# Sixteen gate projections as eight pairs of seven half-size products, with a shared minimum and undivided maps in branch A

## The chip, the cores and the metric

The kernel runs on one core of one Trainium2 chip. The metric is the device time of one execution in microseconds. The engines are named as in the profile: PE multiplies matrices (PEld is its loading of weights), DVE, ACT and POOL work elementwise, SP issues DMAs. A line number such as L735 is a line of the kernel before.

## The reference

An encoder block over 1024 tokens and 16 meta tokens, width 1024, in float32. What matters here:

```
proj = rms_norm(h) @ w_in              # queries, keys, values of A and B, then gates ga and gb (1024 columns each)
# branch A, 4 heads, two maps each, 1040 keys:
attn = softmax(q1 k1^T / 8 + bias) - lam * softmax(q2 k2^T / 8 + bias)
y_a  = rms_norm(attn @ v) * gain
# branch B: 8 heads over a window of 128 keys on either side, plus the meta tokens
merged = sigmoid(ga) * (y_a @ w_ba) + sigmoid(gb) * (y_b @ w_bb)
h = h + merged @ w_o;  h = h + swiglu(rms_norm(h));  out = rms_norm(h)
```

The gates are two products of a 1024 x 1024 activation with a 1024 x 1024 weight. The tokens' bias in branch A is minus a slope times the distance; to the meta tokens the distance counts as zero.

## The kernel before

**Precision.** A float32 operand is split into a high part (ACT, L115) and the rest (POOL or DVE, L116), each in a reduced float format, and a product is three matmuls: high times high, high times rest, rest times high. The activation lies transposed in `hT_hi` and `hT_lo`, eight blocks of 128 features by 1040 tokens.

**Stages.** (1) Input norm and the first projections. (2) The window attention of branch B (`attend_b`, L358 to L406: scores on PE, minimum on DVE, exponential on ACT, the division on POOL at L370, transposes, values), with the projections of branch A's queries, keys and values put between its steps. (3) Branch A with the gates. (4) The branch products (L679), the product with `w_o`, and the feed-forward part.

**Branch A** works through 32 tiles of 128 queries (4 heads of 8). `scores_a` computes, for map 1 and then map 0, three chunks of 352, 352 and 336 keys (two matmuls each, L735), each in its own PSUM bank out of five (`SC`). DVE adds slope times distance and takes the running minimum (L741; the last chunk in two instructions, 16 meta keys and 320 others). ACT takes the exponential with the sum of the row (L746), DVE the reciprocal (L747). POOL scales map 1 by its reciprocal and minus lambda (L749), DVE joins both maps (L752), POOL copies the meta columns (L753). One tile later PE transposes the joined map (L764), ACT and DVE split it (L767, L768), and for every second tile PE multiplies it with the values (L777). `normed_a` squares the result, sums it on PE (L790), and applies the norm (L792 to L799).

**Order.** In stage 3 PE's order is written by hand. Each tile walks through the string `SLOTS`: `s` is one score chunk, `t` one group of transposes, `n` one step of the values or the norm of an earlier pair of tiles, and `g` one gate step, three matmuls of 512 columns. `G_FIRST` gate steps stand ahead of the first tile, `G_HEAD` ahead of the first tile of the three other heads; in both places `load_a` issues the loads of the head's queries, keys and values, whose buffers are single. `HOLD` gate steps are kept for the end: there each call of `step_tail` is followed by `fill(3)`, and `fill(1000)` issues what is left. A gate column block (128 columns by 1024 tokens) is 48 matmuls in two chunks (`project_steps`, L227), copied out by ACT (L686) and stored (L687); its weight is loaded at L188. The order on the other engines comes from a planner that simulates the program. SP issues almost all loads and stores in one order.

## Time and profile before

| what | value |
| --- | --- |
| time of three runs | 1429.1, 1431.18, 1431.73 us; median 1431.18 us |
| profiled execution | span 1427.5 us; the page gives no other time of it, so 1.6 to 4.2 us of the runs' times lie around the span |
| granted TensorE clock | 0.999 |
| stage 2, about | 60 to 293 us |
| stage 3, about | 293 to 621 us (first score matmul at 313.7 us) |
| branch products from | 621.4 us |

A row of a group reads: line, engine, operation, output and inputs, shapes, count, then total busy time and the mean duration of one, then how long the engine was idle before them and for whom. A row of the timeline or of the chain begins with its start and its duration. Matmuls overlap in the pipeline, so the duration of one matmul is not its cost: the distance from start to start is.

### The profile page before, as it was taken

The numbers are of one execution on the slowest core, as the hardware profiler recorded it, in microseconds if no ns is written. First come the engines' busy times: TensorE is split into PE (matmuls) and PEld (weight loads), VectorE is DVE, ScalarE is ACT, GpSimd is POOL, SyncE is SP. The second block draws the span as 40 slices with busy tenths as digits, with TensorE's granted clock in tenths as the row PEclk, the third lists the DMA queues.
The fourth block names the chain that finished last, engine by engine and source line by source line (L and its number), as shares of the span: only waits on it lengthen the run. The fifth ranks groups of instructions, "written<-read, shape, count | busy, mean of one in ns | idle before, by whom it ended". The sixth has DMA issues, their size and how long they took to land.

```text
span 1427.5 us, 20915 instructions
## 1 busy us (share of the span) xinstructions
PE 1418.5 (99%) x7279; PEld 1222.2 (86%) x7279; DVE 907.8 (64%) x1808; ACT 673.0 (47%) x1276; POOL 463.7 (32%) x462
## 2 busy tenths in 40 slices
...
GB/s 240 95 124 104 99 115 106 84 257 48 149 75 157 68 156 68 34 307 242 143 123 82 207 83 145 152 99 104 110 104 96 97 108 99 357 188 141 125 126 148
DMA packets 159018, 191.55 MB, mean 134 GB/s; under 512 B 16104, under 2 KB 103600, under 8 KB 158912
## 3 DMA queue, kind: packets, MB, share of 16 engines
...
q14 instruction: 48, 0.39, 0.1%
...
## 4 chain that ended last, share of the span: by engine, by line
PE 96%; DMA 1%; DVE 1%; issue 0%; ACT 0%; POOL 0%; SPq 0%; DVEq 0%
PE pg L1363 29%; PE pd L1467 15%; PE pp_g L227 12%; PE ppa L679 5%; PE aps L735 4%; PE po L1266 4%; PE apy L777 3%; PE pp_ka L227 3%; PE pp_va L227 3%; PE pp_qb L227 3%; PE pp_qa L227 3%; PE apt L764 2%; PE bps L358 2%; PE po L1274 2%; PE bpy L398 1%; PE bpt L393 1%
## 5 line engine op out<-in xcount | busy, mean ns | idle before, releaser
L1363 PE MATMUL pg<-t,wop 128*128 128x512 f32 x1056 | 242.4, 389 | 0.0
L1363 PEld LDWEIGHTS pg<-t,wop 128*128 128x128 f32 x1056 | 198.3, 188 | 41.1
L1467 PE MATMUL pd<-ob,oa 128*128 128x512 f32 x924 | 209.6, 389 | 0.0
L1467 PEld LDWEIGHTS pd<-ob,oa 128*128 128x128 f32 x924 | 173.5, 188 | 36.0
L116 POOL TENSOR_TENSOR wop<-wf,wop 128x512 fp32r<-128x512 f32 x114 | 150.5, 1320 | 164.7 <-ACT wop L115 154.7
L1363 PE MATMUL pg<-b,wop 128*128 128x512 f32 x792 | 183.3, 389 | 0.0
L1363 PEld LDWEIGHTS pg<-b,wop 128*128 128x128 f32 x792 | 148.5, 188 | 30.7
L116 POOL TENSOR_TENSOR wl_c<-w_c,wh_c 128x1024 fp32r<-128x1024 f32 x32 | 77.4, 2419 | 137.4 <-ACT wh_c L115 115.7
L115 ACT ACTIVATE wop<-wf 128x512 fp32r<-128x512 f32 x128 | 80.8, 632 | 71.7 <-PE pg L1363 50.5
L746 ACT ACTIVATE as<-as,amn 128x1040 f32<-128x1040 f32 x64 | 74.5, 1165 | 73.8 <-DVE amn L741 73.7
L227 PE MATMUL pp_g<-hT_hi,wh_c 128*128 128x512 f32 x256 | 100.9, 394 | 0.0
L227 PE MATMUL pp_g<-hT_lo,wh_c 128*128 128x512 f32 x256 | 100.4, 392 | 0.0
L227 PE MATMUL pp_g<-hT_hi,wl_c 128*128 128x512 f32 x256 | 100.3, 392 | 0.0
L115 ACT ACTIVATE oa<-ra 128x512 fp32r<-128x512 f32 x77 | 48.7, 632 | 108.5 <-PE pd L1467 50.4
L735 PE MATMUL aps<-ak,aq 128*128 128x352 f32 (+1 forms) x384 | 93.0, 327 | 0.3 <-DMA ak<-ka_d 0.3
L116 POOL TENSOR_TENSOR oa<-ra,oa 128x512 fp32r<-128x512 f32 x27 | 34.9, 1294 | 168.6 <-ACT oa L115 167.2
L1140 DVE TENSOR_TENSOR s<-wf,wf 128x512 f32<-128x512 f32 x22 | 18.2, 827 | 110.4 <-DMA wf<-in_w_ff_up_dram 70.2
L735 PEld LDWEIGHTS aps<-ak,aq 128*128 128x128 f32 x384 | 69.7, 188 | 14.4 <-DMA ak<-ka_d 0.7
L741 DVE CUSTOM_DVE_ANT_0 as<-aps,dist,amn 128x352 f32<-128x352 f32 (+1 forms) x128 | 71.3, 564 | 10.4 <-PE aps L735 8.4
L360 DVE CUSTOM_DVE_ANT_0 bs<-bps,tbx,nsink 128x432 f32<-128x432 f32 (+1 forms) x64 | 38.3, 627 | 53.4 <-PE bps L358 28.9
L370 POOL TENSOR_SCALAR bs<-bs,bdn 128x432 f32<-128x432 f32 (+1 forms) x64 | 36.9, 596 | 97.2 <-DVE bdn L368 69.4
L741 DVE CUSTOM_DVE_ANT_0 as<-aps,dist,far_a 128x352 f32<-128x352 f32 x64 | 37.1, 580 | 42.2 <-PE aps L735 42.1
...
## 6 DMA issues: line engine op xcount, KB each, us to landing
...
```

The lines of the kernel that those rows point to most:

```text
L115: high = nc.scalar.activation(hi, src, AF.Copy)
L116: lo_eng.tensor_tensor(lo, src, f32(hi), ALU.subtract)
L227: product = nc.tensor.matmul(ps[:, :n], a[:, c, :], b[:, c, at:at + n], start=(u == 0), stop=(u == 3 * DC - 1))
L360: nc.vector.tensor_tensor_reduce(st[:, r, :W], ps[:, :W], tb, 2.0 ** -(4 * g + r + 1), nsink[:, 4 * g + r:4 * g + r + 1], ALU.add, ALU.min ...
L679: nc.tensor.matmul(ps, w[:, a, j, :], src(j, b, tk), start=(j == 0 and n == 0), stop=(j == 3 and n == 2))
L735: nc.tensor.matmul(ps[:, :n], qs[m][:, t * P:(t + 1) * P], ks[m][:, vv, k0:k0 + n], start=(vv == 0), stop=(vv == 1))
L741: nc.vector.tensor_tensor_reduce(s[m][:, a:b], ps[:, a - k0:b - k0], far_by, slope, low, ALU.add, ALU.min, mn[:, m, i + j:i + j + 1])
L746: nc.scalar.activation(s[m][:, 0:L], s[m][:, 0:L], AF.Exp, bias=low, scale=-1.0, accum_out=dn[:, m:m + 1])
L777: nc.tensor.matmul(py[:, cols], v[:kp, a, k, :], at_[:kp, k, b, :], start=(k == 0 and j == 0), stop=(k == 8))
L1266: nc.tensor.matmul(sets_o[p][u], oa[:, a, u * P:(u + 1) * P], ob[:, b, :], start=(p in (1, 5) and j == 0 and k == 0), stop=(p in (2, 3) an ...
L1363: nc.tensor.matmul(ps, op[:, x, c, :], b[:, y, c, :], start=(p in (1, 5) and c == 0 and n == 0), stop=(p in (4, 2, 3) and c == 3 and n == ...
L1467: nc.tensor.matmul(ps[u], oa[:, a, u * P:(u + 1) * P], ob[:, b, :], start=(p in (1, 2, 5) and j == 0 and k == 0), stop=(p in (2, 3, 4) and ...
```

## The change

**Gates.** Sixteen column blocks become eight pairs. A pair is a product of a 256 x 1024 weight with 1024 tokens; weight and tokens are cut in two both ways, and seven products of half size (12 matmuls of 512 columns each) with sums of blocks replace eight. The first 24 products need the tokens as they are (and one mixed block), the last 32 need the mixed blocks. The mixed blocks of the tokens are computed in stage 2 (`tokens_mixed`), on POOL, with a split each, stored to `t_d`, and loaded into `hT_hi` and `hT_lo` over the old blocks in stage 3 (`turn_into`). Weights are mixed on POOL. Partial sums are kept in SBUF, one per pair goes through `u_d` in memory. Weight blocks are loaded up to twice, through four buffers instead of two.

**Scores.** The first two chunks of a map go to one tile of two banks (`two`, a single buffer) and one instruction of DVE; the last chunk becomes one instruction, with the distances copied beside zeros by POOL (`far_m`). `SC` falls from five to three, `SLOTS` and the numbers of gate steps change.

**Maps.** Map 1 is not scaled by itself. The two maps are joined as map 0 plus map 1 times the scalar minus lambda times sum 0 over sum 1, so the joined map carries the factor sum 0, which the norm removes: its epsilon is multiplied by sum 0 squared.

The core of the diff:

```diff
-SC = 5
+SC = 3
...
-SLOTS = "sgsgsngsgsgstntnt"
-SLOTS_LAST = "sgsgsngsgsstntnt"
+SLOTS = "ssgsgssgsngtntgnt"
+SLOTS_LAST = "ssgsgssgsngtntgnt"
...
-HOLD = 36
+HOLD = 22
...
-G_HEAD = 10
-G_FIRST = 30
+G_HEAD = 6
+G_FIRST = 24
...
+    t_d = [dram.tile([P, 2, 4, 512], F32, name=f"t_d{i}") for i in range(4)]
+    u_d = [dram.tile([P, 512], F32, name=f"u_d{i}") for i in range(8)]
...
-    order += [C_GB + i * P for i in range(8)] + [C_GA + i * P for i in range(8)]
...
+    def tokens_mixed():
+        for c in range(4):
+            x = bpool.tile([P, 4, 512], F32, tag="tmix", name=f"tmix_{c}", bufs=1)
+            x11, x12, x21, x22 = (x[:, i] for i in range(4))
+            def whole(i):
+                at = slice(2 * i, 2 * i + 2)
+                src = [f32(h)[:, 4 * i + c, 0:S].rearrange("p (a n) -> p a n", a=2) for h in (hT_hi, hT_lo)]
+                nc.gpsimd.tensor_tensor(x[:, at], src[0], src[1], ALU.add)
+            def kept(k, t):
+                st = bpool.tile([P, 2, 512], F32R, tag=("wh", "wl")[k % 2], name=f"tst{k}_{c}", bufs=1)
+                split(st[:, 0], st[:, 1], t, nc.gpsimd)
+                nc.sync.dma_start(t_d[k][:, :, c, :], f32(st))
+            whole(0)
+            nc.gpsimd.tensor_tensor(x11, x12, x11, ALU.subtract)
+            kept(0, x11)
+            yield
+            whole(1)
+            nc.gpsimd.tensor_tensor(x12, x22, x12, ALU.subtract)
+            kept(1, x12)
+            yield
+            nc.gpsimd.tensor_tensor(x22, x22, x11, ALU.subtract)
+            kept(2, x22)
+            yield
+            nc.gpsimd.tensor_tensor(x21, x21, x22, ALU.subtract)
+            kept(3, x21)
...
+            with tc.issue_after(scaled[-1].ins):
+                for _ in range(2 if g == 0 and t > 3 else 1):
+                    next(mixing, None)
...
-    def gate_steps():
-        for i in range(16):
-            def g_evac(ps, at, n, i=i):
-                st = gstage.tile([P, 512], F32, tag="g", name="gate_stage", bufs=G_BUFS)
-                nc.scalar.copy(st, ps)
-                nc.sync.dma_start(g_d[i][:, at:at + n], st)
-            ensure(1)
-            col = (C_GB if i < 8 else C_GA) + (i % 8) * P
-            for _ in project_steps(col, Q_CHUNKS, f"g{i}", g_evac):
-                yield
-            ensure(W_BUFS - 1)
...
+    G_COLS = [C_GB + 2 * k * P for k in range(4)] + [C_GA + 2 * k * P for k in range(4)]
+    first_g = [(k, p) for i in (0, 2) for p in (1, 2) for k in (i, i + 1)] + [(k, 6) for k in range(4)]
+    first_g += [(k, p) for k in range(4, 8) for p in (1, 6, 2)]
+    order_g = first_g + [(k, p) for k in range(8) for p in (5, 7, 3, 4)]
+    n_first = len(first_g)
...
+    def load_g():
+        while n_loaded[0] < min(len(loads_g), n_freed[0] + 4):
+            kind, k, i = key = loads_g[n_loaded[0]]
+            p, tag = ((wpool, "w"), (gstage, "w2"))[n_loaded[0] // 2 % 2]
+            n_loaded[0] += 1
+            col = G_COLS[k] + i * P
+            w = raw_g[key] = p.tile([P, DC, P], F32, tag=tag, name=f"wg_{kind}{k}_{i}", bufs=2)
+            with ExitStack() as after:
+                if n_loaded[0] > 4:
+                    after.enter_context(tc.issue_after(keys_a[0].ins))
+                nc.sync.dma_start(w, w_in[:, col:col + P].rearrange("(c p) n -> p c n", p=P))
...
+        if p == 1:
+            src = a11
+        elif p == 2:
+            src, done = a12, ["f"]
+            if k < 4:
+                n_freed[0] += 1
+            else:
+                n_freed[0] += 2
+        elif p == 6:
+            tt(a21, a21, a22, ALU.add)
+            tt(a21, a21, a11, ALU.subtract)
+            src = a21
+            if k < 4:
+                n_freed[0] += 2
+        elif p == 5:
+            src = sums_g[k] = gstage.tile([P, 4, P], F32, tag="s", name=f"s1g_{k}", bufs=1)
+            tt(src, a21, a22, ALU.add)
+        elif p == 7:
+            tt(a21, a11, a21, ALU.subtract)
+            src = a21
+        elif p == 3:
+            tt(a12, a12, a11, ALU.add)
+            tt(a12, a12, sums_g.pop(k), ALU.subtract)
+            src = a12
+        else:
+            src = a22
+            n_freed[0] += 2
+        op = ops_g[n] = wpool.tile([P, 2, 4, P], F32R, tag=("wh", "wl")[n % 2], name=f"wopg_{nm}", bufs=W_BUFS)
+        split(op[:, 0], op[:, 1], src, nc.gpsimd)
...
+    def turn_into(i):
+        d, t = INTO_T[i]
+        for hl, h in enumerate((hT_hi, hT_lo)):
+            with ExitStack() as after:
+                if i == 2:
+                    after.enter_context(tc.issue_after(keys_a[0].ins))
+                nc.sync.dma_start(f32(h)[:, 4 * d:4 * d + 4, HALF[t]], t_d[i][:, hl])
...
+        for n, (k, p) in enumerate(order_g):
+            ensure_g(n + 1)
+            if n == n_first - 4:
+                kept[0] = kept_g("u_0")
+                nc.sync.dma_start(kept[0], u_d[0])
+            if n >= n_first - 1 and p in (2, 4) and (n < n_first or k < 7):
+                nxt = 0 if n < n_first else k + 1
+                banks["next"] = bank(psum2, f"pp{(n + 1) % 2}", f"pg_{nxt}_5", 1)
+                nc.scalar.copy(banks["next"], kept[nxt])
+            op = ops_g.pop(n)
+            if p == 5:
+                banks[5] = banks.pop("next")
+            elif p in (1, 6, 7):
+                banks[p] = bank(psum2, f"pp{n % 2}", f"pg_{k}_{p}", 1)
+            if p in (1, 2):
+                banks[1, k] = banks.get((1, k), banks[1])
+            ps = banks[1, k] if p in (1, 2) else banks[{3: 5, 4: 7}.get(p, p)]
+            d, t = RIGHT_G[p]
+            for c in range(4):
+                for i, (x, h) in enumerate(((0, hT_hi), (0, hT_lo), (1, hT_hi))):
+                    nc.tensor.matmul(ps, op[:, x, c, :], h[:, 4 * d + c, HALF[t]],
+                                     start=(p in (1, 6, 7) and c == 0 and i == 0),
+                                     stop=(p in (2, 6, 3, 4) and c == 3 and i == 2), skip_group_check=True)
+                if c == 3:
+                    if p == 1:
+                        kept[k] = kept_g(f"p1_{k}")
+                        nc.scalar.copy(kept[k], ps)
+                    elif p == 2:
+                        st = stage_g(f"g11_{k}")
+                        nc.scalar.copy(st, ps)
+                        store(st, 2 * k, 0)
+                    elif p == 6:
+                        u = kept.pop(k)
+                        add(u, ps, u, ALU.add)
+                        nc.sync.dma_start(u_d[k], u)
+                    elif p == 5:
+                        kept["q"] = kept_g(f"q_{k}")
+                        nc.scalar.copy(kept["q"], ps)
+                    elif p == 7:
+                        st = stage_g(f"g22_{k}")
+                        add(st, ps, kept.pop("q"), ALU.add)
+                        store(st, 2 * k + 1, 1)
+                    else:
+                        st = stage_g(f"g{p}_{k}")
+                        if p == 3:
+                            nc.scalar.copy(st, ps)
+                        else:
+                            add(st, ps, kept[k], ALU.add)
+                        store(st, 2 * k + (p == 4), int(p == 3))
+                    if n + 1 == n_first - 2:
+                        turn_into(0)
+                    elif n + 1 == n_first - 1:
+                        turn_into(1)
+                    elif n + 1 == n_first:
+                        turn_into(3)
+                    if p == 4:
+                        del kept[k]
+                    if p == 7 and k < 7:
+                        kept[k + 1] = kept_g(f"u_{k + 1}")
+                        nc.sync.dma_start(kept[k + 1], u_d[k + 1])
+                yield
+            ensure_g(n + 4)
...
+    far_m = [apool.tile([P, 336], F32, name=f"far_m{i}") for i in range(2)]
+    for i in range(2):
+        nc.gpsimd.memset(far_m[i][:, S - 704:], 0.0)
...
+        if not h:
+            turn_into(2)
...
+        if t % 4 == 0:
+            sum_a[h, t // 4] = small.tile([P, 4], F32, tag="asum", name=f"asum_{nm}")
+        first_sum = sum_a[h, t // 4][:, t % 4:t % 4 + 1]
         u0 = 896 - t * P
+        nc.gpsimd.tensor_copy(far_m[t % 2][:, 0:S - 704], dist[:, u0 + 704:u0 + S])
         for m in (1, 0):
             s[m] = s0s[t % 2] if m == 0 else apool.tile([P, L], F32, tag="s1", name=f"as1_{nm}", bufs=S_BUFS[1])
-            low = far_a
+            two = psum2.tile([P, 2, 512], F32, tag="two", name=f"aps2_{nm}_{m}", bufs=1)
             for i, (k0, n) in enumerate(A_CHUNKS):
-                ps = bank(psum2, "sc", f"aps_{nm}_{m}_{k0}", SC)
+                ps = two[:, i] if i < 2 else bank(psum2, "sc", f"aps_{nm}_{m}", SC)
                 for vv in range(2):
                     nc.tensor.matmul(ps[:, :n], qs[m][:, t * P:(t + 1) * P], ks[m][:, vv, k0:k0 + n],
                                      start=(vv == 0), stop=(vv == 1))
-                parts = [(k0, min(k0 + n, S), dist[:, u0 + k0:u0 + min(k0 + n, S)])]
-                if k0 + n > S:
-                    parts.insert(0, (S, L, no_dist))
-                for j, (a, b, far_by) in enumerate(parts):
-                    nc.vector.tensor_tensor_reduce(s[m][:, a:b], ps[:, a - k0:b - k0], far_by, slope, low,
-                                                   ALU.add, ALU.min, mn[:, m, i + j:i + j + 1])
-                    low = mn[:, m, i + j:i + j + 1]
+                if i == 1:
+                    nc.vector.tensor_tensor_reduce(s[m][:, 0:2 * n].rearrange("p (a k) -> p a k", a=2), two[:, :, :n],
+                                                   dist[:, u0:u0 + 2 * n].rearrange("p (a k) -> p a k", a=2), slope, far_a,
+                                                   ALU.add, ALU.min, mn[:, m, 0:1])
+                elif i == 2:
+                    nc.vector.tensor_tensor_reduce(s[m][:, k0:k0 + n], ps[:, :n], far_m[t % 2], slope, mn[:, m, 0:1],
+                                                   ALU.add, ALU.min, mn[:, m, 1:2])
                 if i < 2:
                     yield
-            nc.scalar.activation(s[m][:, 0:L], s[m][:, 0:L], AF.Exp, bias=low, scale=-1.0, accum_out=dn[:, m:m + 1])
-            nc.vector.reciprocal(dn[:, m:m + 1], dn[:, m:m + 1])
+            nc.scalar.activation(s[m][:, 0:L], s[m][:, 0:L], AF.Exp, bias=mn[:, m, 1:2], scale=-1.0,
+                                 accum_out=dn[:, 1:2] if m else first_sum)
             if m:
-                (nc.gpsimd if t % 4 in COMBINE_POOL else nc.vector).tensor_scalar(
-                    s[1][:, 0:L], s[1][:, 0:L], dn[:, 1:2], neglam, ALU.mult, ALU.mult)
+                nc.vector.reciprocal(dn[:, 1:2], dn[:, 1:2])
             yield
-        nc.vector.scalar_tensor_tensor(s[0][:, 0:L], s[0][:, 0:L], dn[:, 0:1], s[1][:, 0:L], ALU.mult, ALU.add)
+        nc.vector.tensor_scalar(dn[:, 0:1], first_sum, dn[:, 1:2], neglam, ALU.mult, ALU.mult)
+        nc.vector.scalar_tensor_tensor(s[0][:, 0:L], s[1][:, 0:L], dn[:, 0:1], s[0][:, 0:L], ALU.mult, ALU.add)
...
-        nc.vector.tensor_scalar(f, pst[:, 0:4], 1.0 / P, EPS, ALU.mult, ALU.add)
+        sums = sum_a.pop((h, c))
+        e = small.tile([P, 4], F32, tag="ae", name=f"ae_{nm}", bufs=2)
+        nc.vector.scalar_tensor_tensor(e, sums, EPS, sums, ALU.mult, ALU.mult)
+        nc.vector.scalar_tensor_tensor(f, pst[:, 0:4], 1.0 / P, e, ALU.mult, ALU.add)
...
-    n_gates = [256 - HOLD]
+    n_gates = [4 * len(order_g) - HOLD]
...
-                    ensure(2)
-                    preload(order[0])
+                    ensure_g(2)
...
-        fill(3)
+        fill(1)
```

52 lines of the change are left out of this document (47 added, 5 removed).

## The prediction

> **What bounds the kernel now.** I read the page's shares first, then its chain of what ended last, then the groups of the gate projections, and last the chain in order of time where the gates run alone.
>
> ```profile
> span 1427.5 us, 20915 instructions
> PE 1418.5 (99%) x7279; PEld 1222.2 (86%) x7279; DVE 907.8 (64%) x1808; ACT 673.0 (47%) x1276; POOL 463.7 (32%) x462
> ...
> PE 96%; DMA 1%; DVE 1%; issue 0%; ACT 0%; POOL 0%; SPq 0%; DVEq 0%
> ...
> L227 PE MATMUL pp_g<-hT_hi,wh_c 128*128 128x512 f32 x256 | 100.9, 394 | 0.0
> ```
>
> ```profile
> 293.38 20.45 PE pp_g L227 x90
> ```
>
> PE is the bound: it holds 96% of the chain and never idles before a gate matmul. The gates are three such groups of 256, 768 matmuls. One lasts 394 ns by its group, but 90 in a row take 20.45 us, so the price of one is 20.45 / 90 = 0.2272 us. With the group's mean the gain below would come out 1.7 times too large.
>
> The stage in which the gates run has other engines at work too:
>
> ```profile
> 313.70:581.60 267.90, 267.56 (x1636) 242.90 (x1634) 209.52 (x701) 143.00 (x264) 80.94 (x84) 1.00 0.33 102
> ```
>
> In the 32 tiles' 267.9 us DVE is busy 209.5 (78%), ACT 143 (53%), POOL 81 (30%), at full clock.
>
> **The change, part by part.**
>
> *Matmuls.* 8 pairs x 7 products x 12 = 672 instead of 768: 96 x 0.2272 = **21.8 us less on PE**. Scores, transposes and values keep their counts. No row shows PE waiting for DVE, ACT or POOL in the tiles, so a lighter DVE gives nothing by itself: 21.8 is the ceiling.
>
> *DVE, ACT and POOL inside the stage.*
>
> ```profile
> L741 DVE CUSTOM_DVE_ANT_0 as<-aps,dist,far_a 128x352 f32<-128x352 f32 x64 | 37.1, 580 | 42.2 <-PE aps L735 42.1
> L741 DVE CUSTOM_DVE_ANT_0 as<-aps,dist,amn 128x320 f32<-128x320 f32 x64 | 35.1, 548 | 1.4
> L741 DVE DVE_READ_ACCUMULATOR2_ANT amn<- 128x1 f32 x256 | 20.9, 81 | 0.0
> L741 DVE CUSTOM_DVE_ANT_0 as<-aps,no_dist,amn 128x16 f32<-128x16 f32 x64 | 14.8, 231 | 10.6 <-PE aps L735 7.7
> L768 DVE TENSOR_TENSOR at<-apt,at 128x512 fp32r<-128x512 f32 x64 | 43.5, 685 | 6.9 <-ACT at L767 6.9
> L749 POOL TENSOR_SCALAR as<-as,adn,neglam 128x1040 f32<-128x1040 f32 x32 | 38.9, 1215 | 76.6 <-DVE adn L747 76.6
> ...
> L116 POOL TENSOR_TENSOR wop<-wf,wop 128x512 fp32r<-128x512 f32 x114 | 150.5, 1320 | 164.7 <-ACT wop L115 154.7
> L116 POOL TENSOR_TENSOR wl_c<-w_c,wh_c 128x1024 fp32r<-128x1024 f32 x32 | 77.4, 2419 | 137.4 <-ACT wh_c L115 115.7
> L115 ACT ACTIVATE wop<-wf 128x512 fp32r<-128x512 f32 x128 | 80.8, 632 | 71.7 <-PE pg L1363 50.5
> L686 ACT COPY gate_stage<-pp_g 128x512 f32<-128x512 f32 x32 | 18.4, 576 | 35.7 <-PE pp_g L227 14.1 <-issue 12.4 <-DMA ka_d<-qk_stage 7.9
> L753 POOL COPY as<-as 128x32 f32<-128x32 f32 x32 | 6.7, 210 | 75.6 <-DVE as L752 75.6
> ```
>
> A DVE minimum costs (580 - 548) / 32 = 1.0 ns a column and some 230 fixed. The joint one over 704 columns should take 580 + 352 = 0.93 us, with its read-out 1.01, where two take 1.32. Per tile: two 16-column pieces go (0.62), two joins save 0.62, less 0.03 for wider last chunks: 1.2 us less. Added: three sums of 0.685 per pair, 24 in all, 16.4 us against 38.7. POOL loses L749 (38.9) and sixteen 2.42 us rests, and gets 56 rests and 48 sums of weight blocks at 1.32 each (137 us) and 32 copies of 320 columns (bounded by L753's 0.21 and L749's 1.22; I take 0.5): from 30% to about 55%. ACT gets 56 splits at 0.632 and 40 copies at 0.576, and loses 32 copies and 16 splits of twice the width (at most 1.26 each): at least 20 us more, about 60%. No engine becomes the bound by its sum; PE's cover remains, if each hand-over comes in time.
>
> Costed at nothing: three single banks for five (a tile takes five of them, so one comes round after 4 us or more, and ACT and DVE release it in 0.60 + 0.69), the scalar of the two sums for a reciprocal and the extra term of the norm's epsilon (no wider than L747, behind the same exponential). Also the operands of the products: one is needed every four gate steps, 2.7 us bare, and POOL makes one in 1.3 to 4.0 with four ahead; bare stretches last six products at most, beyond which it would cost up to 1.3 each. And the mixed tokens' second loads: the first is 2 MB, some 7 us at the 296 GB/s shown below, and two products (eight gate steps, a tile and a half or 12 us) lie between the last use of the old block and the first of the new; without that cover it would be 7 us once. What SP has behind them, gate stores and weight loads, has buffers for two to four products.
>
> *The two-bank wait.* The one new wait within a tile: map 0's first chunk needs `two` back from DVE. Behind it on PE stand the whole tile's remaining slots.
>
> ```profile
> 430.07 0.69 PE pp_g L227 x3
> 430.76 0.33 PE aps L735 x2
> ```
>
> Between map 1's second chunk and map 0's first lie two gate steps and one chunk: 0.69 + 0.33 + 0.69 = 1.71 us. DVE needs 1.01 and the matmul's end and two hand-overs, some 0.3 (an estimate from the matmul's 0.39 against its 0.23 pace): a slack of 0.4 us. One L768 (0.69) ahead of it on DVE eats that. Ends: 0 and 0.7 us a tile, 22 us. I take 2, since tiles with value steps (7 to 9 us of PE each) let DVE catch up.
>
> *The four heads' starts.* The keys of map 0 can be loaded only when the last head's last map 0 chunk is done.
>
> ```profile
> 369.26 0.32 PE aps L735 x2
> ...
> 370.95 12.49 DMA ak<-ka_d
> ...
> 383.49 0.43 PE aps L735
> ```
>
> ```profile
> 324.52 1.09 PE apt L764 x9
> ...
> 442.01 0.31 PE aps L735 x2
> ...
> 443.63 1.07 PE apy L777 x9
> ```
>
> ```profile
> 445.02 0.68 SPq L714 DMA_DIRECT2D ak<-ka_d  x1
> ```
>
> ```profile
> DMA to landing us min/median/max: 6.7/9.0/9.1
> ```
>
> At the second head PE was at the edge: 369.58 to 383.49, 13.9 us. At the third the keys landed by 445.02 + 9.1 = 454.1, 11.8 us after the last chunk at 442.32. With the new slots PE has from that chunk on: two gate steps 1.4, nine transposes 1.1, 25 value matmuls 25 / 9 x 1.07 = 3.0, six gate steps 18 x 0.2272 = 4.1, then three chunks and two gate steps 2.4: 11.9 us (rounded once). So the second head waits 2.0, the third nothing, with transfers as fast as before. They will have more beside them: 36 weight loads of 512 KB for 16, 8 MB of mixed tokens, 4 MB for `u_d`. Ends 0 and 9; I take 3.5.
>
> ```profile
> 301.24 0.45 SPq L714 DMA_DIRECT2D ak<-ka_d  x1
> ```
>
> ```profile
> DMA to landing us min/median/max: 6.9/9.4/9.6
> ```
>
> ```profile
> 304.00:308.00 4.00, 4.00 (x19) 3.31 (x18) 0.00 (x0) 1.53 (x2) 2.39 (x1) 1.00 1.06 296
> ```
>
> The first head: its keys landed by 310.8 and the chip's DMA was full (296 GB/s). Two more weight loads ahead of them (1 MB) add 3.4 us: 314.2. Map 0's first chunk now comes at 293.4 + 24 x 0.682 + 2.4 = 312.1: 2 us. The fifth product, at 304.3, needs such a weight split; if it comes behind the keys, up to 8. I take 2 (ends 0 and 8).
>
> *The end of the stage.* Of the 202 gate steps that the tiles may use, 24 + 18 + 160 are gone when the last pass begins, so it holds no gate step.
>
> ```profile
> 588.33 0.60 ACT L767 ACTIVATE at<-apt 128x512 fp32r<-128x512 f32 x1
> ...
> 588.96 0.69 DVE L768 TENSOR_TENSOR at<-apt,at 128x512 fp32r<-128x512 f32 x1 [1.44 <-ACT at L767]
> ```
>
> ```profile
> 608.16 0.44 PE apf L798 x4
> 608.60 12.96 PE pp_g L227 x57
> ```
>
> ```profile
> PEld ppa L679 <- DVE yb L116: 0.5, 1, 0.5
> ```
>
> The last transposes are split in 0.60 + 0.69 us before the values can follow, with two short transposes beside: 1.1 us bare. After the last norm 57 gate matmuls (12.96 us) covered the loads and splits for the branch products, with 0.5 short of it. Now 15 steps are left (22 held back, 9 calls of one each, two of them after the norm), 45 x 0.2272 = 10.2 us: 2.7 bare. Sum 3.8; with what else is late I take 4 (ends 1 and 8).
>
> *Stage 2.* POOL gets 4 x (2 x 2.42 + 8 x 1.32) = 61.6 us, ACT 16 splits (10 us), SP 16 stores.
>
> ```profile
> 202.16 2.42 POOL L370 TENSOR_SCALAR bs<-bs,bdn 128x432 f32<-128x432 f32 x4 [3.99 <-DVE bdn L368]
> ...
> 216.09 2.43 POOL L370 TENSOR_SCALAR bs<-bs,bdn 128x432 f32<-128x432 f32 x4 [2.23 <-DVE bdn L368]
> ```
>
> Divisions come every 13.9 us and, with one wide rest of 2.42 between them, leave some 9 idle. One unit of mixing is 2.6 or 5.1, two of the long ones 10.1: 1 us too much, twice, and PE has projections to put there. I take 0.5 (ends 0 and 6).
>
> **Sum:** -21.8 + 2 + 3.5 + 2 + 4 + 0.5 = -9.8 us in the profiled execution, 1427.5 to 1417.7. What lies around the span stays, so from the median 1431.2 to **1421.4 us**.
>
> **Rivals.**
>
> *DVE late, through POOL (slower).* The joining L752 reads two SBUF operands. Beside a nearly idle POOL it is constant; where POOL runs weight sums, such instructions of DVE are not:
>
> ```profile
> L752 DVE SCALAR_TENSOR_TENSOR as<-as,adn,as x32: 1280/1298/1304, 323.1 to 586.2; 128x1040 f32<-128x1040 f32 x32
> ```
>
> ```profile
> L1411 DVE TENSOR_TENSOR as<-c,as x11: 676/1815/1820, 868.2 to 1213.1; 128x512 f32<-128x512 f32 x11
> ```
>
> That is up to 1.1 us more per tile, landing ahead of the joint minimum. With 0.4 of slack, 0.7 x 32 = 24 us in place of the 2 I took: 1443. It decides from a mean two-bank wait of 0.46 us (14.7 us over 32 tiles, past 1434). Against it: 55% of POOL, so about half the joins collide, and the join falls in the first half of the gap between the minima. [...]
>
> *Almost all is kept (faster).* The transfers come in time and the slots leave no bare spot but the end: -21.8 + 3 = 1412.4. For it: DVE gets lighter and PE had no idle time. Against: the covers counted above shrink on paper.
>
> *Transfers eat it (no change).* First weights behind the keys (8), heads at 9, end 4, mixing 1: -21.8 + 22 = 1431.
>
> **Chances.** Forecast, 1416 to 1428: 0.52. Kept, 1409 to 1416: 0.20. Eaten, 1428 to 1434: 0.10. DVE late, beyond 1434: 0.18. About 0.2% (2.9 us) is what a measurement of this kernel can tell from no change. So faster 0.72, same 0.10, slower 0.18. The range 1410 to 1434 leaves out 0.02 below and 0.18 above; most of the chance has one sign.
>
> **What would show it.** 672 gate matmuls at 0.227 us. PE waiting for L741's successor near nothing in the tiles, and L752's successor spread from 1.28 to 2.4 us. PE idle for keys once or twice, 2 us each; 1 us ahead of the last values; 2 to 3 us ahead of the branch products. Wrong if PE waits for the two banks in most tiles, if it waits for weight splits in the tiles, or if stage 2 ends later than 294 us by more than 2.

## The result, and the profile after

The change makes the kernel slower: 1468.67 us (median of four runs, 1460.98 to 1473.9) against 1431.05 us, a ratio of 1.0261 with a 95% interval of 1.0226 to 1.0297. The prediction said 1421.4 and at most 1434. The profiled execution took 1460.98 us, the shortest of the four, with a span of 1458.9 us: 31.4 more than before. The runs also spread over 13 us where those of the kernel before spread over 3. What the profile shows is therefore the loss of the fastest run, 31.4 us; the medians differ by 37.6, and no profile shows where the other 6 are.

The page of the changed kernel, its shares, the chain's engines, two slices of activity and the groups of gate and feed-forward matmuls:

```profile
PE 1419.6 (97%) x7183; PEld 1209.3 (83%) x7183; DVE 913.6 (63%) x1584; ACT 704.8 (48%) x1340; POOL 603.2 (41%) x591
...
PEclk9999999998999999989999999999999999999999
...
PE 87%; DVE 5%; DMA 4%; ACT 2%; issue 1%; SPq 1%; POOL 0%; ACTq 0%; DVEq 0%; POOLq 0%
...
L1568 PE MATMUL pg<-b,wop 128*128 128x512 f32 x792 | 188.5, 395 | 0.0
L850 PE MATMUL pg<-hT_hi,wopg 128*128 128x512 f32 x448 | 174.7, 410 | 8.5 <-ACT wopg L117 7.8
```

There are 96 matmuls fewer (7183 for 7279) and yet PE is busy longer, 1419.6 us for 1418.5. PE's part of the chain fell from 96% to 87%: for the rest it waited. And a busy PE is a slower one here: its clock row dips, and the feed-forward matmuls on `b`, which the change does not touch, went from 389 to 395 ns. Its row before:

```profile
L1363 PE MATMUL pg<-b,wop 128*128 128x512 f32 x792 | 183.3, 389 | 0.0
```

What PE waited for, us in total, times, longest:

```profile
PE ppa L719 <- ACT yb L117: 7.9, 1, 7.9
PE pg L850 <- ACT wopg L117: 7.8, 2, 6.0
PE aps L939 <- DVE at L972: 6.5, 7, 2.1
PE aps L939 <- DVE amn L942: 3.3, 7, 1.0
PE aps L939 <- DMA ak<-ka_d: 3.2, 3, 1.7
```

In the list of before no wait within this stage is longer than this one:

```profile
PE aps L735 <- DMA ak<-ka_d: 0.3, 1, 0.3
```

Now there is one at each edge: operands of the branch products (the end), gate weights (the start), single score banks, the two-bank tile, keys.

Windows of 3.4 us in the changed kernel, busy us and count of each engine, then PE's granted clock, the DMA share and GB/s:

```profile
304.10:307.50 3.40, 1.59 (x8) 0.90 (x6) 0.00 (x0) 1.13 (x2) 0.42 (x1) 1.00 1.18 299
307.50:310.90 3.40, 2.89 (x8) 2.01 (x7) 0.00 (x0) 1.66 (x4) 3.40 (x4) 0.50 1.03 329
345.10:348.50 3.40, 1.70 (x9) 1.28 (x8) 3.40 (x6) 1.12 (x2) 3.40 (x5) 1.00 0.53 153
348.50:351.90 3.40, 3.40 (x24) 3.09 (x23) 2.79 (x9) 1.88 (x4) 3.40 (x4) 1.00 0.77 230
362.10:365.50 3.40, 1.28 (x7) 0.84 (x6) 3.36 (x6) 1.07 (x3) 2.47 (x4) 1.00 0.17 63
365.60:369.00 3.40, 3.40 (x11) 3.00 (x10) 1.44 (x5) 1.25 (x2) 0.59 (x1) 0.51 0.00 0
```

They go in pairs. Where PE was busy for 1.59 or 1.28 us of a window, the next window ran at half clock (0.50); after 1.70 busy it did not. So a short wait is paid a second time. In all 34.1 us passed at half clock, 29.6 of them within the stage. The others, from the same view:

```profile
307.50:314.30 6.80, 6.29 (x16) 4.64 (x15) 0.00 (x0) 2.24 (x5) 4.56 (x4) 0.50 1.03 301
328.00:338.20 10.20, 6.30 (x20) 5.00 (x21) 3.24 (x5) 3.39 (x8) 8.18 (x7) 0.50 0.84 238
...
508.90:512.30 3.40, 3.40 (x13) 3.11 (x13) 1.85 (x7) 1.35 (x3) 0.07 (x1) 0.50 0.00 0
...
644.37:648.90 4.53, 3.93 (x9) 2.73 (x9) 4.53 (x7) 4.53 (x9) 0.79 (x1) 0.50 1.10 353
```

PE was busy for 6.29 + 6.30 + 3.40 (the stretch at 365.6, above) + 3.40 = 19.4 us of the four ahead of the end. At half clock the gates' matmuls start 0.427 us apart (median, 307 to 314 us), 1.88 times the 0.227 of the kernel before. Half of the 19.4, 9.7 us, is taken as the clock's price within the stage, an estimate (by these two distances it would be 9.1); the last row adds 2.0 in the branch products in the same way.

**Where the 31.4 us are.** From the first gate product to the first branch product: 328.2 us before, 350.2 after (644.37 - 294.16, the starts of two matmuls). That is -21.8 of matmuls, 29.2 more of gaps between them, 9.7 of clock, and 4.9 that no row assigns: +22.0. Before the stage 0.9, in the yb half of the branch products 2.4, in the feed-forward part 6, 5.2 of them in the one group above.

### The profile page after: what moved, and what is told of

The parts are those of the page before. It is cut to its first block, busy times and chain, and to the rows that moved or that the text cites. A ratio compares the mean times of both kernels' runs of the same rounds, so it can differ in the third digit from the quotient of the medians.

```text
span 1458.9 us, 20686 instructions
## 1 busy us (share of the span) xinstructions
PE 1419.6 (97%) x7183; PEld 1209.3 (83%) x7183; DVE 913.6 (63%) x1584; ACT 704.8 (48%) x1340; POOL 603.2 (41%) x591
## 4 chain that ended last, share of the span: by engine, by line
PE 87%; DVE 5%; DMA 4%; ACT 2%; issue 1%; SPq 1%; POOL 0%; ACTq 0%; DVEq 0%; POOLq 0%
PE pg L1568 29%; PE pd L1672 14%; PE pg L850 6%; PE ppa L719 5%; PE po L1471 4%; PE aps L939 3%; PE pp_va L228 3%; PE pp_qb L228 3%; PE pp_qa L228 3%; PE apy L981 3%; PE pp_ka L228 3%; DMA ak<-ka_d 2%; PE bps L395 2%; PE po L1479 2%; PE bpy L435 1%; PE bpt L430 1%
## 5 line engine op out<-in xcount | busy, mean ns | idle before, releaser
L1568 PE MATMUL pg<-b,wop 128*128 128x512 f32 x792 | 188.5, 395 | 0.0
L850 PE MATMUL pg<-hT_hi,wopg 128*128 128x512 f32 x448 | 174.7, 410 | 8.5 <-ACT wopg L117 7.8
L850 PEld LDWEIGHTS pg<-hT_hi,wopg 128*128 128x128 f32 x448 | 87.0, 194 | 22.4 <-ACT wopg L117 8.5
L939 PE MATMUL aps<-ak,aq 128*128 128x352 f32 (+1 forms) x384 | 88.5, 338 | 13.1 <-DVE at L972 6.5
L939 PEld LDWEIGHTS aps<-ak,aq 128*128 128x128 f32 x384 | 66.2, 192 | 30.7 <-DVE at L972 7.9
L942 DVE CUSTOM_DVE_ANT_0 as<-aps,dist,far_a 128x704 f32<-128x704 f32 x64 | 60.4, 944 | 48.2 <-PE aps L939 48.2
L850 PE MATMUL pg<-hT_lo,wopg 128*128 128x512 f32 x224 | 89.9, 402 | 0.0
L1595 ACT COPY p<-pg 128x512 f32<-128x512 f32 x44 | 25.8, 585 | 66.5 <-PE pg L1568 62.3
L981 PE MATMUL apy<-at,av 128*128 128x256 f32 x400 | 57.4, 287 | 0.0
```

The costliest lines, as they stand in the source:

```text
L850: nc.tensor.matmul(ps, op[:, x, c, :], h[:, 4 * d + c, HALF[t]], start=(p in (1, 6, 7) and c == 0 and i == 0), stop=(p in (2, 6, 3, 4) and ...
L939: nc.tensor.matmul(ps[:, :n], qs[m][:, t * P:(t + 1) * P], ks[m][:, vv, k0:k0 + n], start=(vv == 0), stop=(vv == 1))
L942: nc.vector.tensor_tensor_reduce(s[m][:, 0:2 * n].rearrange("p (a k) -> p a k", a=2), two[:, :, :n], dist[:, u0:u0 + 2 * n].rearrange("p ( ...
L981: nc.tensor.matmul(py[:, cols], v[:kp, a, k, :], at_[:kp, k, b, :], start=(k == 0 and j == 0), stop=(k == 8))
L1568: nc.tensor.matmul(ps, op[:, x, c, :], b[:, y, c, :], start=(p in (1, 5) and c == 0 and n == 0), stop=(p in (4, 2, 3) and c == 3 and n == ...
```

## The experiments

All were timed over three rounds. "Stage" is from the first gate product to the first branch product, "gaps" the time between matmuls in it, "half" the time at half clock from 293 to 712 us, each of the profiled run and worked out from its matmul and clock records. "Clock's price" in the text is half of the time that PE was busy at half clock in the stage, the estimate made above.

| kernel | median us | ratio to before (95%) | stage | gaps | half |
| --- | --- | --- | --- | --- | --- |
| before | 1431.05 | 1 | 328.2 | 0.3 | 0 |
| the change | 1468.67 | 1.0261 (1.0226 to 1.0297) | 350.2 | 29.5 | 34.1 |
| scores alone | 1438.12 | 1.0049 (1.0034 to 1.0064) | 335.2 | 5.0 | 0 |
| gates alone | 1451.68 | 1.0143 (1.0128 to 1.0158) | 344.7 | 27.6 | 23.9 |
| same addresses | 1456.75 | 1.0180 (1.0158 to 1.0202) | 352.7 | 35.4 | 27.3 |
| weights early | 1460.68 | 1.0211 (1.0194 to 1.0228) | 347.9 | 29.0 | 23.9 |
| splits first | 1450.77 | 1.0134 (1.0100 to 1.0168) | 335.7 | 19.6 | 13.7 |
| clock kept up | 1453.73 | 1.0158 (1.0141 to 1.0174) | 348.9 | 16.6 | 6.8 |
| gates repaired | 1448.44 | 1.0118 (1.0093 to 1.0144) | 345.8 | 28.2 | 27.3 |
| gates, whole maps | 1440.23 | 1.0058 (1.0041 to 1.0075) | 337.3 | 24.0 | 13.7 |
| whole maps alone | 1430.58 | 1.0003 (0.9993 to 1.0012) | 328.0 | 0.1 | 0 |
| all repaired | 1445.68 | 1.0105 (1.0088 to 1.0122) | 337.4 | 19.5 | 10.2 |
| best parts | 1444.66 | 1.0101 (1.0086 to 1.0116) | 334.7 | 18.0 | 17.1 |
| weights spread | 1445.23 | 1.0096 (1.0081 to 1.0112) | 340.9 | 24.9 | 20.5 |
| best again | 1446.01 | 1.0107 (1.0080 to 1.0134) | 337.7 | 19.5 | 13.7 |
| no mixing | 1437.54 | 1.0048 (1.0033 to 1.0063) | 331.3 | 18.8 | 13.7 |
| fewer loads | 1441.31 | 1.0072 (1.0057 to 1.0087) | 334.8 | 21.5 | 13.7 |
| both left out | 1436.76 | 1.0049 (1.0035 to 1.0062) | 333.8 | 21.5 | 17.1 |
| cover kept | 1441.64 | 1.0073 (1.0056 to 1.0090) | 337.0 | 19.3 | 17.1 |
| change with cover | 1448.04 | 1.0119 (1.0104 to 1.0134) | 343.1 | 24.1 | 13.7 |

Two theories stood against each other at first. **Supply and order**: the gate weights come late at the stage's start and the operands of the branch products at its end. **Score tiles**: the two-bank tile and the three single banks make PE wait. Two more factors were to be priced beside them, the clock and the addresses.

### The two halves of the change

```diff
 scores alone: the kernel before, with
+two = psum2.tile([P, 2, 512], F32, tag="two", ..., bufs=1)
+SC = 3; SLOTS = "ssgsgssgsngtntgnt"; far_m; asum, ae; maps undivided
 gates alone: the changed kernel, with
-two-bank tile, SC = 3, undivided maps, new SLOTS
+one minimum for each bank, SC = 5, maps divided at once, old SLOTS
```

> The kernel before, with the score part of the change alone: the two-bank minimum, the far copies, maps left undivided, three single banks for five, the new order of slots; its gates are the old ones, in whole products. Unused tiles of 64 bytes keep the addresses of the large tiles as they stood before, modulo 128. If the waits for score tiles are what the change lost (in the changed kernel's list of waits: 3.3 us for the two-bank minimum and 6.5 us for a single bank, with the half clock that follows some of them), this kernel is 8 to 16 us slower than before, about 1439 to 1447 us, and shows those waits by the same names. If the loss lies in the supply of gate weights and in the end of the stage, it is within 4 us of 1431, since the old gate products fill the engine. If VectorE was short before, it is a little faster, by up to 3 us: its minima fall from three to two for each map.

> The changed kernel with the old score part: one minimum per bank, five single banks, maps divided at once, the old slots. Only the gates in seven half-size products are new. 96 matmuls of 0.2272 us less are 21.8 us. If the supply of weights, the end of the stage and the clock after each gap carry the loss (11 us of waits at the stage's start, 8 at its end, some 10 of half clock), it comes to 1431 - 22 + 25 to 35, that is 1434 to 1444 us, and the gaps at 305, 325 and 636 us of the changed kernel are there again. If the score tiles carry it, the gates alone give 1413 to 1420 us. [...]

Both lose: 8.0 us the scores, 21.5 the gates (1438.12 and 1451.68 against 1430.15). Neither theory alone was right, and the sum, 29.5, is close to the 26.6 of the whole change at equal addresses (next experiment). The scores come out 0.9 us below the range that the score tiles had been given. PE's waits with the scores alone:

```profile
PE aps L745 <- DVE at L778: 3.1, 3, 1.2
PE aps L745 <- DVE amn L748: 1.9, 5, 0.4
```

They are the two names expected, at half the size, perhaps because old gate products still fill PE; no half clock follows, and no window of 3.41 us has more than 1.4 us of idle time. The rest lies in the stage beside these gaps (2.3) and in the yb half of the branch products (2.0, of which 1.4 are waits for yb). With the gates alone:

```profile
PE pg L852 <- ACT wopg L117: 8.5, 2, 6.6
PE ppa L721 <- ACT yb L117: 7.1, 1, 7.1
PE apt L961 <- DVE as L949: 4.0, 4, 2.5
PE aps L932 <- DMA ak<-ka_d: 2.4, 2, 2.0
PE apt L961 <- DVE adn L944: 2.3, 1, 2.3
```

Start and end are there again; in the middle the transposes wait for joins, as they do not in the kernel before. The time is past the upper end that supply and order gave for it (1444). It fits a third theory, that POOL's mixing slows DVE's join and makes scores late in every head, at 1440 us or more: the join's mean is 1562 ns here against 1297 before, 8.5 us over 32 tiles. Scores late in every head are not seen. The experiment without mixing, below, puts a bound on this term.

### Addresses

```diff
+const.tile([P, 16], F32, name="left_pad")
+acon.tile([P, NM], F32, name="right_pad")
```

> The changed kernel with two unused tiles of 64 bytes, one on each side of the SBUF, and nothing else: the large tiles stand again at multiples of 128 bytes, as before the change; in the changed kernel they stood 64 bytes off. If the address of the moving operand sets the duration, the 792 matmuls of the feed-forward part that read the b tiles fall from 395 to 389 ns and that part is 4 to 5 us shorter; the gates' and the scores' matmuls, whose tiles stood 64 bytes off too, fall by as much, 672 and 384 of them, some 4 to 6 us more: 1457 to 1462 us by the median of 1468.7. If the address has nothing to do with it, no matmul's mean changes and the time is within 3 us of the changed kernel's.

The group of the feed-forward part, in this kernel:

```profile
L1570 PE MATMUL pg<-b,wop 128*128 128x512 f32 x792 | 183.2, 389 | 0.0
```

From 395 back to 389 ns, 188.5 to 183.2 us: 5.3 us that came from 64 bytes of small tiles laid below the large ones. The `b` tiles stood at byte 2880 of a partition and are now at 2944 (2688 before), 64 and 0 modulo 128; these are the addresses that the built programs give them. The group on `t`, whose moving tiles did not move, kept 389 in all three.

The other half of the expectation failed. `hT_hi` and `hT_lo` stood 64 bytes off as well, and yet the gates' matmuls at full clock last 391 to 392 ns at the median with the offset and 390 to 392 without. So the offset alone does not slow a matmul; what sets the `b` tiles apart is open. The medians differ by 11.9 us, more than this term, while the two profiled spans differ by 1.4; the changed kernel's profile is that of its fastest run, and how much of the rest is spread between runs is open.

### The start: earlier weights

```diff
+lent = apool.tile([P, 9, 2, 256], F32R, tag="at", ...)   # weight blocks 3 to 6
-ensure_g(2)
+ensure_g(4)
 ...
         keys_a.append(last)
         if not h:
+            load_g(6)
             turn_into(2)
+            load_g(8)
```

> The changed kernel with the first gate weights loaded earlier: the third and fourth block go into a map tile that is idle then, ahead of the keys, and the weights of the first mixed products (the sixth of the first four blocks) go ahead of the token halves and the values. If the supply of weights makes the gaps at 305 and 325 us, both go (3.3 and about 7.8 us), and with them the half clock that followed (about 8 us of them at half speed lost 3.4 and 5.1): 1452 to 1459 us for a median of 1468.7. If the gaps only change their names, because the keys or the token halves land later by what the weights took, the sum of the tensor engine's waits before 335 us stays within 3 us and so does the time.

What happened at the start of the changed kernel, on SP, POOL and PE:

```profile
312.23 4.69 SPq L755 DMA_DIRECT2D wg_m<-in_w_in_dram  x2
```

```profile
327.56 1.27 POOL L779 TENSOR_TENSOR wg_m<-wg_m 128x512 f32<-128x512 f32 x1
328.90 2.16 POOL L780 TENSOR_TENSOR wg_m<-wg_m,wg_m 128x512 f32<-128x512 f32 x1
```

```profile
331.78 0.80 PE L850 MATMUL pg<-hT_hi,wopg 128*128 128x512 f32 x1 [6.01 <-ACT wopg L117]
```

The first mixed product needs two blocks loaded anew. They were issued from 312.23 on, behind keys, token halves and values, landed at 325.0 and 326.7, were summed twice by POOL and split by ACT and POOL; PE stood for 6.01 us, and its first matmul then took 0.80 us, at half clock.

With earlier weights the waits for weight splits fall from 8.3 to 1.3 us, but those for keys grow from 3.2 to 5.1, and new ones for copies by ACT come up (2.9 + 0.8). The median falls by 8.0 (1468.67 to 1460.68), to just above the range of supply and order. The two profiled runs show less: they differ by 1.9 us, their gaps by 0.5, and the gaps ahead of 335 us fall from 8.5 to 6.1 only, which is what the rival had named; 10 us of half clock are gone. So the late weights are shown as a wait, and their price of 8 us rests on the medians alone.

### The end: ScalarE's order

```diff
+        with tc.issue_after(yb_last.ins):      # the same for the split of the third branch weight
             gate_ops.append(nc.scalar.activation(gt, gt, AF.Sigmoid))
```

> The changed kernel at the old addresses (the third experiment) with one edit: ScalarE's first four gate sigmoids, and the split of the third branch weight, are queued behind the eight splits of the yb operand, where in the changed kernel they stand ahead of it and wait 4.7 us for gates that have only just been stored. If that order makes the 9.6 us for which the tensor engine waits for yb, the wait falls to 1 to 4 us, the half clock after it (13.7 us in the third experiment) to 7 or less, and the time to 1446 to 1451 us, against 1456.8. If the loads of yb are what is late, because the sync engine's queue has stores of gates between them, the wait stays above 7 us under the name of a DMA or of the same splits, and the time at 1454 to 1458.

ACT at the end of the changed kernel:

```profile
640.38 2.72 ACT L1196 ACTIVATE gt<-gt 128x512 f32<-128x512 f32 x4 [4.72 <-DMA gt<-g_d]
643.17 0.63 ACT L117 ACTIVATE wbhb<-wbrb 128x512 fp32r<-128x512 f32 x1
643.71 4.25 ACT L117 ACTIVATE yb<-m 128x512 fp32r<-128x512 f32 x8
```

The sigmoids stand ahead of the yb splits and wait for gates that were still on their way to memory. With the splits first, the waits for yb fall from 10.2 us (9.6 for ACT, 0.6 for DVE, at the same addresses) to 2.7, and the half clock around them from 13.7 to 3.4. The longest that is left:

```profile
PE ppa L724 <- DVE yb L119: 2.1, 3, 1.2
```

The median falls by 6.0 to 1450.77, within the expected range. The runs spread over 12 us and overlap with those without the edit, so the 6.0 is rough; the profiled run is the shortest of the four here, so its stage (335.7) flatters it.

### The clock

```diff
+for _ in range({4: 6, 8: 30}.get(n, 0)):      # and 40 ahead of the first branch product
+    nc.tensor.matmul(ps, hT_hi[:, 4, 0:P], hT_hi[:, 4, 0:512], start=True, stop=True)
```

> The changed kernel at the old addresses, with matmuls whose results are overwritten put into three gaps: 6 ahead of the fifth gate product, 30 ahead of the ninth, 40 ahead of the first branch product, about as much as the tensor engine idles there (1.5, 7.3 and 9.6 us at 0.227 each). The waits themselves stay. If the granted clock halves because of the idle stretch, the half-clock stretches at 326 and 640 us (6.8 and 13.7 us) vanish, the first branch products take 390 ns instead of 800, and the time falls by what ran at half speed after the gaps, 1.8 + 3.8 us and the like: 1449 to 1453 us against 1456.8. If the clock drops for another reason (the transfers, the other engines), the stretches stay where they are and the time is the same or, where the added matmuls outlast the gap, 1 to 3 us longer.

PE at the end, with the 40 added matmuls, and the windows around it:

```profile
633.99 9.23 PE L1205 MATMUL ppa<-wbhb 128*128 128x512 f32 x40
643.06 0.39 PE L721 MATMUL ppa<-yb,wbhb 128*128 128x512 f32 x1
```

```profile
640.00:650.00 10.00, 8.58 (x37) 6.46 (x36) 7.31 (x11) 9.30 (x18) 2.31 (x2) 1.00 1.07 374
```

The same stretch of the kernel without them:

```profile
640.00:653.60 13.60, 6.94 (x16) 5.04 (x17) 7.55 (x12) 10.43 (x19) 2.54 (x2) 0.50 1.04 368
```

Transfers and the other engines are no less busy with the added matmuls, and only PE's idle time has gone (1.42 of 10 us for 6.66 of 13.6): with it the granted clock was 0.50, without it 1.00, so here it followed PE's own idleness. The first branch product takes 0.39 us again, for 0.79 at the same addresses without them. The median falls by 3.0 us to 1453.73, just above the expected range, and by less than the runs of one kernel spread; two windows with idle time that was not filled (2.6 and 1.9 us) were still followed by 3.4 us at half clock each.

### Which part pays

```diff
 gates repaired: gates alone + weights early + splits first
 gates, whole maps: the same, and
-                (nc.gpsimd if t % 4 in COMBINE_POOL else nc.vector).tensor_scalar(s[1]..., neglam, ...)
+        nc.vector.tensor_scalar(dn[:, 0:1], first_sum, dn[:, 1:2], neglam, ALU.mult, ALU.mult)
 whole maps alone: the kernel before with that edit
```

> The gates alone (old score part), with the early weights and with the splits of yb ahead of the sigmoids. The gates alone gave 1451.7 us with 9.1 us of waits for weights, 7.6 for yb, 6.3 for maps, 4.7 for keys and tiles, and 24 us at half clock. If weights and the order at the end carry their loss, some 8 and 6 us of waits go and the half clock after them, about 5 us, and it comes to 1430 to 1436 us. If POOL's weight mixing, queued ahead of the division of the maps, carries it, the waits for the maps stay at 6 us or grow and it is 1438 to 1446.

> As the repaired gates, with one part of the score change added: the maps are left undivided until the norm (the join takes the undivided maps, GpSimd divides none), while each score bank keeps its own minimum and the five single banks stay. If GpSimd's queue (mixing of weights ahead of the maps' division) makes the joins late, the waits for maps go, and this is 4 to 8 us below the repaired gates, 1423 to 1430 us: the part of the change that pays, without the two-bank tile. If VectorE itself was late in those tiles, it is within 2 us of the repaired gates.

> The kernel before with undivided maps alone: the join takes undivided maps, GpSimd divides none, the norm's epsilon is scaled; old gates, one minimum for each bank, five single banks. The score part as a whole cost 7.9 us. If the two-bank tile and the three single banks made that, this one is within 2 us of before (1429 to 1433 us) and shows no wait of the tensor engine over 1 us in the stage. If the undivided maps make the join late (they need both sums first), 1434 us or more with waits of the transposes for the join.

The repairs were worth 3.2 us instead of 15 or more, above both ranges: the yb wait stayed (7.2 us), because a split of ya, whose data come later, had slipped ahead of those of yb on ACT. The undivided maps are worth 8.2 us beside the gates (1448.44 to 1440.23) and nothing by themselves (1.0003). With them the transposes' waits for joins fall from 7.0 to 1.3 us. That POOL, which mixes weights there, is what they relieve fits this but is argued: no run divides the maps without mixing beside the new gates. Since they are free by themselves, the 8.0 us of the scores alone are the price of the two-bank tile, its slots, the copies of distances and the three single banks; these were not separated.

### Repairs together

```diff
 all repaired: the whole change, same addresses, weights early, splits first (also ahead of ya), and
-G_HEAD = 6; G_FIRST = 24
+G_HEAD = 10; G_FIRST = 26
 best parts: gates, whole maps, with the same two edits
 weights spread: gates, whole maps, with each mixed product of the first four pairs ahead of a later pair
 best again: weights spread, G_HEAD = 8, G_FIRST = 26, one split of ya behind those of yb
```

> The whole change at the old addresses, with every repair so far: weights early, the yb splits ahead of the sigmoids (and of the splits of ya), and ten gate steps ahead of each head's scores again, for six (26 for 24 ahead of the first). The split-first kernel gave 1450.8 us; the early weights were worth 8 us by themselves and the waits for a head's keys 2 to 4. If supply and order are all that the change lost beside the score tiles, 1437 to 1444 us, the rest being the waits on the two-bank tile and the three single banks (10 us by their names). If those waits grow when the others go, because the score tiles and not the weights set the pace, 1446 to 1452.

> Gates in half-size products, undivided maps, one minimum for each bank with five banks, and the repairs: early weights, the splits of yb ahead of sigmoids and of ya, ten gate steps ahead of each head. The kernel without the last two gave 1440.2 us, with 6.9 us of waiting for yb (a split of ya stood ahead of it on ScalarE), 8.5 us for keys, and 14 us at half clock. If these are order alone, some 6 + 4 us of waits and 3 to 4 of half clock go: 1426 to 1431 us, at or just below the kernel before. If the transfers themselves are late (keys, gates and weights share the DMA engines), the waits move to other names and it stays at 1434 to 1439.

> The gates with whole maps and the first repairs (1440.2 us), with one edit: the sixth products of the first four blocks, each of which needs two weight blocks anew for 2.7 us of matmuls, stand no longer one behind the other but each ahead of the three products of a later block, so that in that stretch 1 MB of weights is asked for every 11 us or so, and not 4 MB within 11 us. The DMA engines were 97% busy from 293 to 345 us there, 57% before the change. If the rate of the transfers is what makes the start late, the waits between 325 and 355 us (5.3 us in four gaps) fall below 2 us and the half clock at 318 with them: 1433 to 1437 us. If the total of the data is what counts, or GpSimd's mixing, they only move: 1438 to 1443.

> The same with the end in order: the first split of ya behind the splits of yb on ScalarE (the other three are left, since moving them all made branch A's first weights 2.7 us late), and eight gate steps ahead of each head, 26 ahead of the first, which is as many as there are without leaving the last tiles without any. If the pieces add up (6.9 us of waiting for yb, 3 of half clock, 2 to 4 for keys): 1425 to 1431 us, which would be level with the kernel before or just below it. If each wait that goes lets another come up, since the transfers are the common limit: 1434 to 1439.

None came out as its gain; the last three lie above both of their ranges. "All repaired" (1445.68) lies between the two forecasts: the waits for score tiles did not grow (6.0 + 3.6 us, against 6.5 + 3.3), but 10.2 us at half clock and new waits for weights and branch operands stayed. In "best parts" the keys' wait fell from 8.5 to 1.4 and yb's to 2.1, as expected, and these took their place:

```profile
PE pg L862 <- ACT wopg L118: 3.3, 2, 2.9
PE pg L862 <- ACT g L871: 3.0, 1, 3.0
PE ppa L725 <- DVE wbha L119: 2.7, 1, 2.7
```

1444.66 is 4.4 us worse than without the two edits: the gaps of the stage fell by 6.0 us, but the clock's price rose from 3.4 to 6.4, and the wait for `wbha`, which lies behind the stage, came with half clock of its own. Spreading the demand for weights did not help either (1445.23): the keys, behind the same weights, waited 9.1 us. Whatever is repaired, 18 to 25 us of gaps remain.

### Is it the mixing, or the loads?

```diff
 no mixing: gates, whole maps, with each product taking a raw block
-            tt(a21, a21, a22, ALU.add)
-            tt(a21, a21, a11, ALU.subtract)
 ...
 fewer loads: gates, whole maps, and
-6: [("m", k, 0), ("m", k, 1)]
+6: [("m", k, 1)]
 ...
-            turn_into(2)
```

> The gates with whole maps and the first repairs (1440.2 us), without GpSimd's additions of the weights: each product takes a raw block instead of a mixed one, so the gates' values are others, while the splits, the loads and the matmuls stay. GpSimd was busy 24 us of the 52 from 293 to 345 us, 15 before the change. [...] If the transfers make them late, it stays within 3 us: 1437 to 1443.

> The same kernel (1440.2 us) with 4 MB less to load at the start of the stage: the first mixed products take one block where they took two, and the first token half is not turned into its mixed form, so the gates' values are others; all matmuls, splits and additions stay. The DMA engines were 97% busy from 293 to 345 us there at some 286 GB/s, so 4 MB are 14 us of them. If the transfers are what the start waits for, the waits between 313 and 352 us (7 us in five gaps) fall below 2 and the time by 5 to 9, to 1431 to 1435 us. If not, it stays at 1437 to 1443.

> Both left out, the additions on GpSimd and the 4 MB of loads; the values are others. If the two losses are separate, the gains of the two runs add up. If both only serve one late product, the sum is that of the larger one. If neither counts, and the tensor engine's waits come from the chain of score tiles with fewer gate matmuls to cover it, it is still above 1434 us.

Had the mixing made the products late, leaving it out was to save 5 us or more (1435 or below). Without mixing the median is 2.7 us lower, without 4 MB of loads 1.1 higher, without both 3.5 lower, and the intervals of all three overlap with that of the kernel they start from. So neither sets the pace there. The mixing does slow the join: its mean is 1508 ns with it and 1360 without, but the time gains no more than those 2.7 us. In all three the same two edges remain; with both left out:

```profile
PE aps L943 <- DMA ak<-ka_d: 8.2, 6, 1.9
PE ppa L725 <- ACT yb L118: 7.1, 1, 7.1
PE apt L972 <- DVE as L960: 4.1, 3, 2.8
```

Transposes wait for joins here too, though POOL neither mixes weights nor divides maps.

### The saved work as cover

```diff
-HOLD = 22; G_HEAD = 6; G_FIRST = 24; SLOTS = "sgsgsngsgsgstntnt"   # five gate steps a tile; the whole change has a string of its own
+HOLD = 36; G_HEAD = 10; G_FIRST = 30; SLOTS = "sgsgsngsgsstntnt"   # four
-    fill(1)
+    fill(3)
```

> The gates with whole maps and the first repairs (1440.2 us), with one thing changed: where the gate work stands. The 96 matmuls that the products save are 32 steps of three, and the change took exactly these 32 from the places where gates cover a boundary: 30 to 24 steps ahead of the first head, 10 to 6 ahead of each other head (12 in all), 36 to 22 kept for the end, while each tile kept its five. Here the boundaries have 30, 10 and 36 again, and the tiles four steps for five. If the saved work was lost because it had covered waits at the boundaries, the 8.5 us of waits for keys and the 6.9 for yb fall below 3 us together, the half clock there goes, and the time is 1418 to 1428 us, faster than before. If the tiles themselves need the fifth step to cover the chain from scores to maps, waits of the transposes and of the scores for VectorE and GpSimd take their place, each tile some 0.3 to 0.7 us, and the time is 1436 us or more.

> The whole change (two-bank minimum, three single banks) at the old addresses, with early weights and the yb splits first, and the same places for the gate steps: 30 ahead of the first head, 10 ahead of each other, 36 at the end, four in each tile. The kernel with all repairs and five in each tile gave 1445.7 us. If the boundaries are what the saved work had covered, 1428 to 1437 us with the score tiles' waits (9.6 us) left; if the two-bank tile and the three banks need the five steps, those waits grow to 15 us or more and it is 1444 us or more.

The waits at the heads and at the end went, as the theory of cover had it: no wait for keys is left, and yb costs 2.3 us. But the time did not follow (1441.64 against 1440.23). PE's longest waits now:

```profile
PE apt L978 <- DVE as L966: 5.5, 4, 2.7
PE pg L862 <- ACT wopg L118: 4.2, 1, 4.2
PE pg L862 <- ACT g L871: 3.0, 1, 3.0
PE apt L978 <- POOL as L967: 3.0, 3, 2.0
```

By place, the gaps before and after the edit are: from the first gate product to the first transposes of branch A 3.8 and 9.0 us, from there to the last scores 12.8 and 7.6, behind these 7.5 and 2.7. So the start lost, where 30 steps now run through more products before the first tile and wait for weights; the tiles and the end gained. The sum of the gaps fell by 4.7 us, and the clock's price took 4.3 back (from 3.4 to 7.7): 13.7 of the 17.1 us at half clock lie ahead of 354 us. The time came out as the rival had said (1436 or more), but its reason is not shown: of the 8.5 us of waits for joins, 3.6 fall into the first tiles and 2.7 behind the last scores, and none of the others is over 0.7.

The whole change with this cover, 1448.04, is no better than with five steps (1445.68). It differs from that kernel in one more thing, a split of ya that stands ahead of yb's again. Its waits for score tiles are 9.4 us, not the 15 that the rival had named; here too the start lost (gaps of 8.9 us for 5.5 up to the first transposes).

## Why the prediction was wrong

**Right.** The price of a matmul and the count: -21.8 us of work went. The joint minimum took 944 ns (0.93 forecast), stage 2 ended 0.9 us later (0.5), the heads' keys cost 3.2 us by name (3.5), the two-bank wait 3.3 (2). For the keys and the two banks the waits carry the names that the prediction gave them. Of the prediction's signs of being wrong only weight splits came, and ahead of the tiles or in the first ones: the loss lay at edges that it had named and priced too low.

**The first step that failed: the first head and its weights, 2 us.** The text saw that the fifth product's split might come behind the keys (up to 8) and took the low end; and it costed the operands of the products at nothing, "with four ahead". Four ahead covers POOL's sums, not two blocks queued behind keys, token halves and values. The waits for weight splits, near 305 and 326 us, were 8.3 us in all (ACT 7.8, POOL 0.5), and with them came 6.8 + 10.2 us at half clock. The experiment with earlier weights took 7.0 us of these waits away and lowered the median by 8.0, though the profiles show only 1.9 of that.

**The end, 4 us (ends 1 and 8).** The bare stretches were counted on PE; the wait of 8.5 us (7.9 + 0.6) came from ACT's queue, where the sigmoids stood ahead of the splits. In the kernel before the splits came first:

```profile
617.75 0.63 ACT L115 ACTIVATE yb<-m 128x512 fp32r<-128x512 f32 x1
...
625.44 2.19 ACT L991 ACTIVATE gt<-gt 128x512 f32<-128x512 f32 x4
```

That order is written nowhere in the code; the planner chooses it, and it chose another one here (what turned it was not tried). Moving the sigmoids took 7.5 us of waits away and lowered the median by 6.0.

**Three single banks for five, at nothing.** The text took the time until a bank comes round, but not that transposes and scores now share three: 6.5 us of waits by name, and with the two-bank tile 8.0 us as a whole in the kernel with the scores alone.

**What was not in the sum at all.** The clock: 9.7 us in the stage and 2.0 behind it, a second price on five windows of 3.41 us with 1.67 to 2.24 us of idle time. The addresses: 5.3 us in a stage that the change does not touch. The sum had counted every wait at full clock, and no stage behind the gates.

**The rivals.** "DVE late, through POOL" would have been slower, 1443 (its 0.7 x 32 is 22.4 and not 24, which makes it 1442), but it is not what made the loss. Its join did spread, and as far as it had said, to 2.4 us:

```profile
L956 DVE SCALAR_TENSOR_TENSOR as<-as,adn,as x32: 1287/1302/2407, 324.1 to 613.1; 128x1040 f32<-128x1040 f32 x32
```

The median is that of before, the mean 1398 ns for 1297: 3.2 us over 32 tiles, on an engine that is 63% busy, and the two-bank waits that it was to feed are 3.3 us. What stretches a join is not shown. In the kernel before, the seven slow additions of L1411 (1.81 to 1.82 us) had a rest of POOL (L116, not a weight sum) beside them for 1.27 us, the four others (0.68 to 0.69) for 0.19 at most. In the changed kernel five joins took 1.46 to 2.41 us, each with work of POOL beside it, but ten others with 0.83 to 1.35 us of it beside them took 1.30 to 1.31. In the kernels with single banks the join is slower still (1562 ns with the gates alone, 1508 with whole maps), and leaving out the mixing gained 2.7 us. "Transfers eat it" was nearest in kind: it gave the first weights 8 us, the heads 9 and the end 4, and the waits are 8.3, 3.2 and 8.5. The first two late blocks did take 12.8 and 13.1 us to land; but the wait at the end came from the order on ACT, and leaving out 4 MB of loads, tried in the kernel with early weights, gained nothing. Fewer loads behind the start were not tried.

**The common cause.** 21.8 us is 32 gate steps, and the change's own numbers show whence it took them: 30 to 24 ahead of the first head, 10 to 6 three times, 36 to 22 at the end, 6 + 12 + 14 = 32. The prediction counted each of these covers by itself and found each long enough but for some 2 or 3 us. What the runs show is that this work was the cover itself at the heads and at the end: with it back there, the waits for keys went from 8.5 us to none and those for yb from 6.9 to 2.3. What they do not show is a place that could spare it. With 30 steps ahead of the first head the start ran out of weights, and the clock took the gain. A kernel with all of the cover at the heads and the end but 24 steps at the start was not run, nor one step less in the tiles by itself. No gate version here came below 1440 us at the median without leaving out part of its work. It stays open whether one exists.
